# Attention's outputs stored in whole rows and put in order by the loads, in a hybrid decoder block

## The chip, the cores and the metric

The kernel runs on one core of a Trainium2 chip. The metric is the device time of one execution in microseconds; the median of several runs is compared. Five engines work side by side, each through its own list of instructions in order: PE (TensorE, matrix products), DVE (VectorE), ACT (ScalarE), POOL (GpSimd) and SP (SyncE), which in this kernel does nothing but issue DMA transfers. A transfer is carried out by the core's 16 DMA engines, in packets of one contiguous run of bytes each. An engine that needs another's result waits for a semaphore, and what stands behind the waiting instruction on the same engine waits with it.

## The reference

One block of a decoder for 1024 tokens of width 1024. An input projection feeds two groups of heads: eight heads of stick-breaking attention (64 wide) and four heads of a gated delta rule (128 wide). Both outputs are normed per head, gated, joined and multiplied by the output projection; the residual and a last norm follow.

```
def stick_breaking_attention(q, k, v):
    ...
        causal = s_idx[None, :] < t_idx[:, None]
        sp = jnp.where(causal, jax.nn.softplus(z), 0.0)
        tail = lax.cumsum(sp, axis=sp.ndim - 1, reverse=True) - sp
        attn = jnp.where(causal, jnp.exp(jax.nn.log_sigmoid(z) - tail), 0.0)
        outs.append(jnp.einsum('bhqk,bhkd->bhqd', attn.astype(v.dtype), vb))

def reference(x, norm1_w, w_in, ...):
        h = rmsnorm(x, norm1_w[layer])
        proj = jnp.einsum('btd,de->bte', h, w_in[layer])
        ...
        o_sb = rmsnorm(o_sb.transpose(0, 2, 1, 3), sb_norm_w[layer]).reshape(b, t_len, SB_WIDTH)
        o_sb = o_sb * jax.nn.silu(sb_z)
        qkv = jax.nn.silu(causal_depthwise_conv(jnp.concatenate([g_q, g_k, g_v], axis=-1), gdn_conv_w[layer]))
        ...
        o_gdn = gated_delta_chunked(gq, gk, gv, decay, beta)
        ...
        mixed = jnp.concatenate([o_sb, o_gdn], axis=-1)
        x = x + jnp.einsum('bte,ed->btd', mixed, w_out[layer])
    return rmsnorm(x, final_norm_w)
```

## The kernel before

**A planner lays out every queue.** While the kernel is built, `Model` (lines 174 to 345) keeps a clock of its own. Each instruction that the program records gets a price (`cost`, line 398), the instructions whose results it needs, and a rank `prio`: the lower, the sooner it is taken among those that are ready on its engine (`start`, line 301). A transfer costs SP 475 ns in this account, and its packets are priced by their length (line 404). The orders so found are fixed with dependencies at the end of `block`, so on the chip each engine keeps to the planner's order, whether or not the planner's times come true. Line 363 is the line of the helper that records, which is why nearly every row of the profile bears it; rows are told apart by their tiles. `interleave` (line 445) picks which of some twenty streams goes on next; each has a rank for its instructions (line 1638 on: DELTA 0, WEIGHTS 2, BANK 5, WINDOW 10, OUTPUT 12, RESULT 20).

**The stages.** First the queries and half of the values are projected straight from the loads. Then three things run interleaved on PE: the rest of the projections (`projections`, in the order of line 29), attention in windows of 256 tokens (`window`, line 1327: eight heads, four windows each), and the delta rule. After the projections and attention come the products with the output weights: first with the half of the weights that belongs to the delta rule (`products_delta`), then with that of attention (`products_attention`), each in eight blocks of 128 tokens.

**Attention's output.** A window ends with its output turned: 128 values (two partial sums of 64) by 256 tokens. VectorE adds the high and low halves (`o2`), transposes it in 32 by 32 squares into `oe` (line 1407; two buffers), and four stores (line 1409) finish the transposition by writing each square to its place in `o_s`, laid out token by token. Each store covers 32 partitions in runs of 128 bytes. The values of the next head, `v2a`, are loaded into a single buffer (line 1325), and the next head's `q2`, `kh`, `kl` likewise (line 1309).

**The end of attention.** `out_norm` (line 1415) loads a block of 128 tokens of all heads from `o_s` into `both`, 4 KB per token in one piece, for two blocks at a time (the fixed place sg3 cut in two); adds the two partial sums, squares, sums and raises to the power -0.5 on POOL with the tile `half`. `enter_attention` scales the block and gives the place back. `prepare(0)` has PE transpose the block, multiplies by the gate and splits it into a high and a low part (`mm`, shown as mmf); four of these fit. `products_attention` multiplies.

**Convolution.** `g_evac` (line 878) takes a projected bank of q, k or v of the delta rule, copies it with three columns ahead of it into `pre` (two buffers): zeros at the first half of the tokens, the last three columns of the first half at the second. Then come four taps, a sigmoid and a product. For heads 2 and 3 (TURNED is 2) the result is also transposed on VectorE into `pre` and stored by four transfers of 128-byte runs into `gt_s`. These transfers have the rank of the projections' stream, RESULT.

Of the kernel before, what the change touches and what calls it, by code (L numbers as in the profile page):

```python
# [10 lines left out]
F32 = mybir.dt.float32  # L11
F32R = mybir.dt.float32r
I32 = mybir.dt.int32
AF = mybir.ActivationFunctionType
# [3 lines left out]
P = 128  # L18
T = 1024
# [3 lines left out]
SBH = 8  # L23
# [10 lines left out]

OUT_WEIGHTS, DELTA, WEIGHTS, BANK, WINDOW, OUTPUT, RESULT, DECAYS = -1, 0, 2, 5, 10, 12, 20, 25


SAME = 130  # L40
# [438 lines left out]
def block(tc, xT_d, x_d, n1_d, wE_d, wQ_d, wC_d, conv_d, alog_d, dtb_d, mixw_d, wo_d, fnw_d, out_d):  # L479
    nc = tc.nc  # L480
    ck = Model({"V": nc.vector, "A": nc.scalar, "G": nc.gpsimd, "P": nc.tensor, "S": nc.sync})
    V, A, G, TE, S = ck.V, ck.A, ck.G, ck.P, ck.S

    with ExitStack() as top:
        top.enter_context(tc.manual_schedule(engines={mybir.EngineType.PE}))

        def open_pool(name, space="SB", ctx=top, before=(), **kw):
            if space != "SB":
                kw["space"] = getattr(bass.MemoryType, space)
            return Pool(ck, ctx.enter_context(tc.tile_pool(name=name, bufs=1, **kw)), space, before)  # L490

        fx = Fixed(ck, nc, {**{f"sg{w}": (2048 * (w + 1), 1) for w in range(4)}, "o2": (1024, 1), "kq": (4096, 4), "ak": (4096, 4)})
        cst = open_pool("cst")
        dr = open_pool("dr", "DRAM")
        ps = open_pool("ps", "PSUM")
# [12 lines left out]
        step = stepr.bitcast(F32)  # L508
# [4 lines left out]
        rstd = cst.tile([P, NB], F32, name="rstd")  # L513
        rs8 = cst.tile([P, NB], F32, name="rs8")
        ns8 = cst.tile([P, NB], F32, name="ns8")
        half = cst.tile([P, SBH], F32, name="half")
        V.memset(half, -0.5)
        norms = cst.tile([P, 2, 2, 4], F32, name="norms")
        root = cst.tile([P, 4], F32, name="root")
# [2 lines left out]
        def rsqrt(y, a, n):  # L522
            return G.tensor_tensor(y, a, half[:, 0:n], ALU.pow)
# [10 lines left out]
        gate_s = dr.tile([NK, P, T], F32, name="gate_s")  # L534
        g_s = dr.tile([GH, 3, P, T], F32, name="g_s")
        gt_s = dr.tile([GH, 3, T, P], F32, name="gt_s")
        o_s = dr.tile([T, SBH, P], F32, name="o_s")
        og_s = dr.tile([NB, P, GH, P], F32, name="og_s")
        rs_s = dr.tile([NB, P], F32, name="rs_s")
        cum_s = dr.tile([2, GH, NB, P], F32, name="cum_s")  # L540
# [83 lines left out]
        for tag, bufs in (("kh", 1), ("kl", 1), ("q2", 1), ("v2a", 1), ("sg2", 1), ("cc", 2), ("cc", 2), ("sg3", 1)):  # L624
            if tag[0] == "s":
                chl.append(fx.tile([P, 2, 520], F32R, "chl", tag))
            else:
                t = at_.tile([P, 1040 + (48 if tag == "kl" else 0)], F32R, tag=tag, bufs=bufs, name="chl")
# [15 lines left out]
        raw, loads = [], {}  # L644
        for k in range(NK):
            w = s0.tile([P, 512], F32, tag="wcr", bufs=6, name="wq")
# [76 lines left out]
        def first(f, *args, bank=BANK, **kw):  # L723
            ck.prio, prio = bank, ck.prio
            f(*args, **kw)
            ck.prio = prio
# [49 lines left out]
        flags = {}  # L776
# [101 lines left out]
        def g_evac(h, kind):  # L878
            wv = conv[:, 4 * kind + h, :]
            last = []  # L880

            def evac(pt, half):
                pre = gd.tile([P, 515], F32, tag="pre", bufs=2, name="pre")
                if half == 0:
                    V.memset(pre[:, 0:3], 0.0)
                else:
                    A.activation(pre[:, 0:3], last[0][:, 512:515], AF.Copy)
                last.append(pre)
                first(A.activation, pre[:, 3:515], pt, AF.Copy)
                ac = pr.tile([P, 512], F32, tag="kt", bufs=2, name="ac")  # L890

                first(A.activation, pt, pre[:, 0:512], AF.Copy, scale=wv[:, 0:1])
                for i in range(1, 4):
                    first(V.scalar_tensor_tensor, ac if i == 3 else pt, pre[:, i:i + 512], wv[:, i:i + 1], pt, ALU.mult, ALU.add)
                sg = pre[:, 0:512]
                first(A.activation, sg, ac, AF.Sigmoid)
                first(G.tensor_tensor, ac, ac, sg, ALU.mult)
                ts = slice(half * 512, half * 512 + 512)
                if h < TURNED:
                    return S.dma_start(g_s[h, kind, :, ts], ac)  # L900
                done = [S.dma_start(g_s[h, kind, :, ts], ac)] if kind < 2 else []
                first(V.transpose, sg, ac)
                turned = gt_s[h, kind, ts, :].rearrange("(b r) d -> r b d", r=32)
                return done + [S.dma_start(turned[:, :, 32 * a:32 * a + 32], sg[32 * a:32 * a + 32, :].rearrange("r (b c) -> r b c", c=32)) for a in range(4)]

            return evac

# [75 lines left out]
        def delta_pre():  # L983
            yield from decays(pre)
            for h in range(GH):
                for g in range(2):
                    u = 2 * h + g
                    yield from until(f"l{u}g")
                    yield from gdn_pre(h, g)
# [304 lines left out]
        def attention():  # L1294
            yield lambda: "v1" in flags and "dec" in flags
            for i in range(2):
                ccs.append(at_.tile([P, T + 1], F32, tag="cc", bufs=2, name="cc"))
                V.memset(ccs[i][:, T:T + 1], 0.0)
            for h in range(SBH):
                yield lambda: f"k{h // 2}" in flags  # L1300
                kh = at_.tile([P, 1040], F32R, tag="kh", name="kh")[:, 16:1040]
                kl = at_.tile([P, T], F32R, tag="kl", name="kl")
                q2 = at_.tile([P, T], F32R, tag="q2", name="q2")
                i, r = h // 2, slice((h % 2) * 64, (h % 2) * 64 + 64)
                loads = []

                twice = lambda a: a[r, :].unsqueeze(1).to_broadcast([SBD, 2, T])
                for t, src in ((q2, qk_s[i, :, r, :].rearrange("n d t -> d n t")), (kh, twice(qk_s[4 + i, 0])), (kl, twice(qk_s[4 + i, 1]))):
                    loads.append(S.dma_start(t.bitcast(F32), src.bitcast(F32)))
                hd[h] = (q2, kh, kl)  # L1310
                yield loads
                for w in range(4):
                    tok = f"w{w}"
                    yield lambda: busy[tok] == 0 and len([1 for v in busy if v[0] == "w" and busy[v]]) < WINDOWS
                    busy[tok] = 1
                    yield Stream(window(h, w, tok), 10 + 0.01 * (4 * h + w), WINDOW + 0.01 * (4 * h + w))
                    yield lambda: f"s{h}{w}" in flags
            yield lambda: f"e{SBH - 1}3" in flags
# [8 lines left out]
        def window(h, w, tok):  # L1327
# [3 lines left out]
            for i in range(2):  # L1331
                b = 2 * w + i
                end = (b + 1) * P
                sg = sg2[:, i, :]
                cc = ccs[i][:, T - end:T + 1]
                cuts = (0, 384, end) if end == 640 else (*range(0, end, 512), end)
                for s0, s1 in list(zip(cuts, cuts[1:]))[::-1]:
                    n = s1 - s0
# [19 lines left out]
            for j in range(w + 2):  # L1358
                if j <= w:
# [3 lines left out]
                    n = len(blocks)  # L1363
# [11 lines left out]
                    r = V.tensor_tensor(al, src, ah.bitcast(F32), ALU.subtract)  # L1375
# [13 lines left out]
                ahl, r = parts[j - 1]  # L1389
                ov2 = ov.rearrange("p (m t) -> p m t", m=2)  # L1390
                yield r
                for s in (2 * (j - 1), 2 * (j - 1) + 1):
                    i0 = 0 if s <= 2 * w else 1
                    c = slice(256 * (s % 2), 256 * (s % 2) + (1 if i0 else 2) * P)
# [7 lines left out]
            o2 = fx.tile([P, 256], F32, "o2", "o2")  # L1402
# [2 lines left out]
            busy["po"] = 0  # L1405
            oe = at_.tile([P, 256], F32, tag="oe", bufs=2, name="oe")
            V.transpose(oe, o2)
            rows_o = o_s[256 * w:256 * w + 256, h].rearrange("(b r) d -> r b d", r=32)
            flags[f"e{h}{w}"] = [S.dma_start(rows_o[:, :, 32 * a:32 * a + 32], oe[32 * a:32 * a + 32].rearrange("r (b c) -> r b c", c=32)) for a in range(4)]
            yield  # L1410


# [2 lines left out]
        def out_norm(n):  # L1415
            yield lambda: f"e{SBH - 1}3" in flags and fx.room("sg3")
            if n == 0:
                fx.part("sg3", 4096)
            for b in range(n, NB, 2):
                yield lambda: fx.room("sg3")  # L1420
                both = fx.tile([P, SBH, 2, SBD], F32, "both", "sg3")
                ck.hold(both)
                yield S.dma_start(both.rearrange("p h u d -> p (h u d)"), o_s[b * P:(b + 1) * P].rearrange("t h d -> t (h d)"))
                o, spare = both[:, :, 0, :], both[:, :, 1, :]
                V.tensor_tensor(o, o, spare, ALU.add)
                A.activation(spare, o, AF.Square)
                ss = at_.tile([P, SBH], F32, tag="oss", bufs=2, name="oss")
                V.tensor_reduce(ss, spare, AX.X, ALU.add)
                V.tensor_scalar(ss, ss, 1.0 / SBD, EPS, ALU.mult, ALU.add)
                rsqrt(ss, ss, SBH)  # L1430
                normed[b] = both, o, ss
                yield
# [203 lines left out]
        pre = Stream(delta_pre(), 0.7, DELTA + 0.7)  # L1636
# [43 lines left out]
```

## Time and profile before

| what | value |
|---|---|
| median of 3 runs | 636.03 us (634.78 to 637.17) |
| the profiled execution | 639.53 us |
| its span, first to last instruction | 637.8 us |
| mean granted clock of PE | 0.994 |
| DMA packets; mean rate | 165563; 188 GB/s |
| packets under 512 bytes | 96448 |
| share of the 16 engines' time on SP's queue | 62.3% |

The span lies inside the execution's time; the rest, 1.7 us, is ahead of the first and behind the last instruction. Rows give an engine, a line, an operation, the tile written and the tiles read (`o_s<-oe` is a transfer from the tile oe into o_s; a trailing f marks a tile at a fixed place). "SPq" is SP's issuing; a transfer's landing is told apart from it. PE's time is split in PE (products) and PEld (loading the stationary operand), which overlap. In PE's rows a matmul's end is modelled, so that neighbours overlap.

How the 16 DMA engines and the engines are filled over 40 slices of 16 us (tenths, 9 is 90% or more):

```profile
PE   8999999999999999999999989999999999999995
...
DVE  4379973322797798887797696777889774478754
ACT  6665567724786776775785866666777653232553
POOL 0124047728794696881679684386764325245522
...
DMA  8958337856557466598668768453652578984322
```

### The profile page before, as it was taken

How to read it: one execution, taken by the hardware profiler on the slowest of the kernel's cores; microseconds unless marked ns; L12 is line 12 of the kernel's file. 1: busy time of each engine (PE TensorE's matmuls, PEld its weight loads, DVE VectorE, ACT ScalarE, POOL GpSimd, SP SyncE). 2: the span in 40 equal slices, each digit the busy share in tenths (PEclk: the TensorE clock that was granted, in tenths of full speed). 3: DMA queues.
4: the chain of work that ended last, by engine and by line, in shares of the span. 5: the costliest groups of instructions: out<-in, count | busy, mean ns of one | idle time of the engine just before them, and what ended most of it. 6: DMA issues, size and time to landing. Idle time of an engine off the chain costs nothing.

```text
span 637.8 us, 11259 instructions
## 1 busy us (share of the span) xinstructions
PE 624.0 (98%) x3672; PEld 528.7 (83%) x3672; DVE 447.5 (70%) x810; ACT 393.9 (62%) x945; POOL 341.2 (53%) x429
## 2 busy tenths in 40 slices
PE   8999999999999999999999989999999999999995
PEld 7889988988888888788888777888888888888884
DVE  4379973322797798887797696777889774478754
ACT  6665567724786776775785866666777653232553
POOL 0124047728794696881679684386764325245522
PEclk9999999999999999999999999899999999999998
DMA  8958337856557466598668768453652578984322
GB/s 305 342 183 312 124 131 253 303 189 222 159 151 224 131 185 134 141 207 221 167 146 224 185 133 264 121 185 94 180 141 84 151 201 255 311 319 143 116 100 100
DMA packets 165563, 120.21 MB, mean 188 GB/s; under 512 B 96448, under 2 KB 131456, under 8 KB 165504
## 3 DMA queue, kind: packets, MB, share of 16 engines
q1 hardware_dynamic: 165216, 119.29, 62.3%
q8 instruction: 29, 0.48, 0.3%
q14 instruction: 30, 0.25, 0.1%
q10 hardware_dynamic: 288, 0.20, 0.1%
HBM read 80.22 MB, written 39.23 MB: 187 GB/s over the span
## 4 chain that ended last, share of the span: by engine, by line
PE 81%; DMA 6%; ACT 4%; DVE 3%; SPq 2%; issue 2%; POOL 1%; POOLq 0%; DVEq 0%; ACTq 0%
PE pp L363 52%; PE pz L363 21%; PE po L363 6%; PE pc L363 3%; SPq L363 2%; DVE cc L363 1%; DMA v2a<-v_s 1%; DMA kh<-qk_s 1%; DMA xr1f<-xT 1%; DMA o_s<-oe 1%; ACT sgf L363 1%; POOL ac L363 1%; DMA qk_s<-sqh 1%; ACT pz L363 1%; DMA cb<-cum_s 1%
## 5 line engine op out<-in xcount | busy, mean ns | idle before, releaser
L363 PE MATMUL pp<-xh,weh 128*128 128x512 f32 x360 | 146.4, 407 | 0.4 <-DVE ac L363 0.4
L363 PE MATMUL pp<-xh,wel 128*128 128x512 f32 x360 | 141.8, 394 | 0.0
L363 PE MATMUL pp<-xl,weh 128*128 128x512 f32 x360 | 141.3, 392 | 0.0
L363 POOL TENSOR_TENSOR sgf<-sgf,cc 128x128 f32<-128x128 f32 (+3 forms) x64 | 77.5, 1216 | 57.7 <-DVE cc L363 52.5
L363 POOL TENSOR_TENSOR wel<-wer,weh 128x512 fp32r<-128x512 f32 x48 | 62.5, 1305 | 72.0 <-ACT weh L363 71.6
L363 PEld LDWEIGHTS pp<-xh,wel 128*128 128x128 f32 x360 | 68.0, 189 | 15.3
L363 PEld LDWEIGHTS pp<-xh,weh 128*128 128x128 f32 x360 | 68.1, 189 | 12.8 <-DVE ac L363 0.9
L363 PEld LDWEIGHTS pp<-xl,weh 128*128 128x128 f32 x360 | 68.1, 189 | 11.5
L363 DVE TENSOR_TENSOR_SCAN cc<-pz,step 128x384 f32<-128x384 f32 (+2 forms) x64 | 53.4, 844 | 10.6 <-ACT pz L363 9.5
L363 ACT ACTIVATE sgf<-pz,rs 128x384 f32<-128x384 f32 (+3 forms) x96 | 53.5, 593 | 7.6 <-PE pz L363 7.6
L363 DVE TENSOR_TENSOR ahl<-pz,ahl 128x512 fp32r<-128x512 f32 (+1 forms) x80 | 49.5, 630 | 12.0 <-ACT ahl L363 11.3
L363 ACT ACTIVATE ahl<-pz 128x512 fp32r<-128x512 f32 (+1 forms) x80 | 43.2, 559 | 20.6 <-PE pz L363 20.1
L363 ACT ACTIVATE pz<-pz,ns 128x384 f32<-128x384 f32 (+3 forms) x96 | 52.5, 576 | 0.0
L363 PE MATMUL po<-ahl,v2a 128*128 128x512 f32 (+1 forms) x160 | 48.9, 400 | 2.4 <-DMA v2a<-v_s 2.3
L363 PE MATMUL pp<-wo,mmf 128*128 128x512 f32 x192 | 45.5, 396 | 0.0
L363 DVE SCALAR_TENSOR_TENSOR pp<-pre,conv,pp 128x512 f32<-128x512 f32 x42 | 31.4, 747 | 18.2 <-ACT pp L363 17.8
L363 PEld LDWEIGHTS pp<-wo,mmf 128*128 128x128 f32 x192 | 35.8, 188 | 8.4
L363 PE MATMUL pp<-woh,mmf 128*128 128x512 f32 (+2 forms) x136 | 41.9, 385 | 0.0
L363 DVE TENSOR_TENSOR_SCAN cc<-pz,cc,step 128x512 f32<-128x512 f32 (+1 forms) x32 | 38.8, 1211 | 4.1 <-ACT pz L363 3.0
L363 POOL TENSOR_TENSOR mmf<-mgf,mmf 128x512 fp32r<-128x512 f32 x16 | 21.9, 1366 | 37.0 <-ACT mmf L363 23.9
L363 POOL TENSOR_TENSOR ac<-ac,pre 128x512 f32<-128x512 f32 x24 | 31.0, 1293 | 16.3 <-ACT pre L363 10.9
L363 DVE TENSOR_TENSOR xr<-pp,xr 128x512 f32<-128x512 f32 (+2 forms) x33 | 22.2, 672 | 23.0 <-PE pp L363 23.0
(317 smaller groups left out, 1513.9 us busy)
## 6 DMA issues: line engine op xcount, KB each, us to landing
wer<-wE SPq DMA_DIRECT2D x48, 256.0 KB, 3.5
xr<-x SPq DMA_DIRECT2D x16, 512.0 KB, 7.6
g_s<-ac SPq DMA_DIRECT2D x20, 256.0 KB, 2.3
v_s<-v2e SPq DMA_DIRECT2D x16, 256.0 KB, 3.3
kqf<-g_s SPq DMA_DIRECT2D x16, 256.0 KB, 4.0
v2a<-v_s SPq DMA_DIRECT2D x8, 512.0 KB, 5.9
q<-qk_s SPq DMA_DIRECT2D x8, 512.0 KB, 4.5
kh<-qk_s SPq DMA_DIRECT2D x8, 512.0 KB, 3.9
```

Source lines behind the costliest of these rows:

```text
L363: ins = f(*args, **kw).ins
```

## The change

Five edits. (1) `o_s` becomes four windows by eight heads by 128 by 256, and a window's `oe` is stored in one transfer with rows of 1 KB; the squares are no longer put in their places there. (2) `out_norm` loads a block by four transfers, each into 32 partitions with runs of 128 bytes, which finish the transposition; the add behind them waits for all four. (3) The three columns of zeros in `pre` are written by ScalarE, as a copy of three zero columns of `step`, and no longer by VectorE's memset. (4) For heads 2 and 3 the stores of the convolved result and of its transposition get the rank STORES, 1. (5) The tile `half` moves to a fixed place of 32 bytes.

```
-OUT_WEIGHTS, DELTA, WEIGHTS, BANK, WINDOW, OUTPUT, RESULT, DECAYS = -1, 0, 2, 5, 10, 12, 20, 25
+OUT_WEIGHTS, DELTA, STORES, WEIGHTS, BANK, WINDOW, OUTPUT, RESULT, DECAYS = -1, 0, 1, 2, 5, 10, 12, 20, 25
...
-        fx = Fixed(ck, nc, {**{f"sg{w}": ...
+        fx = Fixed(ck, nc, {"half": (32, 1), **{f"sg{w}": ...
...
-        half = cst.tile([P, SBH], F32, name="half")
+        half = fx.tile([P, SBH], F32, "half", "half")
...
-        o_s = dr.tile([T, SBH, P], F32, name="o_s")
+        o_s = dr.tile([4, SBH, P, 256], F32, name="o_s")
...
                 if half == 0:
-                    V.memset(pre[:, 0:3], 0.0)
+                    A.activation(pre[:, 0:3], step[:, 0:3], AF.Copy)
...
                 if h < TURNED:
                     return S.dma_start(g_s[h, kind, :, ts], ac)
+                ck.prio, prio = STORES, ck.prio
                 done = [S.dma_start(g_s[h, kind, :, ts], ac)] if kind < 2 else []
                 first(V.transpose, sg, ac)
                 turned = gt_s[h, kind, ts, :].rearrange("(b r) d -> r b d", r=32)
-                return done + [S.dma_start(turned[:, :, 32 * a:32 * a + 32], sg[32 * a:32 * a + 32, :].rearrange("r (b c) -> r b c", c=32)) for a in range(4)]
+                done += [S.dma_start(turned[:, :, 32 * a:32 * a + 32], sg[32 * a:32 * a + 32, :].rearrange("r (b c) -> r b c", c=32)) for a in range(4)]
+                ck.prio = prio
+                return done
...
             V.transpose(oe, o2)
-            rows_o = o_s[256 * w:256 * w + 256, h].rearrange("(b r) d -> r b d", r=32)
-            flags[f"e{h}{w}"] = [S.dma_start(rows_o[:, :, 32 * a:32 * a + 32], oe[32 * a:32 * a + 32].rearrange("r (b c) -> r b c", c=32)) for a in range(4)]
+            flags[f"e{h}{w}"] = S.dma_start(o_s[w, h], oe)
...
-                yield S.dma_start(both.rearrange("p h u d -> p (h u d)"), o_s[b * P:(b + 1) * P].rearrange("t h d -> t (h d)"))
+                loads = []
+                for q in range(4):
+                    at = 32 * (4 * (b % 2) + q)
+                    loads.append(S.dma_start(both[32 * q:32 * q + 32].rearrange("p h u d -> p (h u d)").rearrange("p (n c) -> p n c", c=32),
+                                             o_s[b // 2, :, :, at:at + 32].rearrange("h (a r) c -> r (h a) c", r=32)))
+                yield loads
```

More of the change, by code (lines that the diff above doesn't have):

```diff
@@ L490, in open_pool @@
             return Pool(ck, ctx.enter_context(tc.tile_pool(name=name, bufs=1, **kw)), space, before)
-        fx = Fixed(ck, nc, {**{f"sg{w}": (2048 * (w + 1), 1) for w in range(4)}, "o2": (1024, 1), "kq": (4096, 4), "ak": (4096, 4)})
+        fx = Fixed(ck, nc, {"half": (32, 1), **{f"sg{w}": (2048 * (w + 1), 1) for w in range(4)}, "o2": (1024, 1), "kq": (4096, 4), "ak": (4096, 4)})
         cst = open_pool("cst")
```

## The prediction

> **What bounds the kernel now.** I read the page's head and its chain first, then PE's waits, then the stretches in which PE is not full.
>
> ```profile
> span 637.8 us, 11259 instructions
> ...
> PE 624.0 (98%) x3672; PEld 528.7 (83%) x3672; DVE 447.5 (70%) x810; ACT 393.9 (62%) x945; POOL 341.2 (53%) x429
> ...
> PE 81%; DMA 6%; ACT 4%; DVE 3%; SPq 2%; issue 2%; POOL 1%; POOLq 0%; DVEq 0%; ACTq 0%
> ```
>
> PE is busy for 624.0 of 637.8 us and holds 81% of the chain that ends last. The change removes no matmul, so at most 13.8 us of idle PE can be won, and not all of that. Where the idle time lies is told by the busy time by stretches (columns: PE, PEld, DVE, ACT, POOL, clock, DMA share, GB/s) and by PE's own waits:
>
> ```profile
> 360.00:400.00 40.00, 35.81 (x257) 29.48 (x258) 29.43 (x53) 26.93 (x75) 27.40 (x32) 0.98 0.77 207
> ...
> 600.00:638.00 38.00, 31.21 (x150) 25.53 (x148) 19.63 (x39) 17.68 (x39) 10.87 (x14) 0.95 0.24 97
> ...
> 398.00:400.00 2.00, 1.95 (x6) 1.66 (x7) 1.37 (x4) 1.98 (x6) 0.51 (x3) 0.65 1.07 289
> 400.00:402.00 2.00, 2.00 (x6) 1.52 (x6) 1.59 (x3) 2.00 (x6) 0.92 (x2) 0.50 0.85 237
> ...
> PE po L363 <- DMA v2a<-v_s: 2.3, 1, 2.3
> PE pz L363 <- ACT wy L363: 1.5, 1, 1.5
> PE pz L363 <- DVE cc L363: 0.6, 2, 0.4
> ```
>
> 6.8 us of it (38.00 - 31.21) is the end, in which the last rows are normed and written; the change does not touch that. 4.2 us (40.00 - 35.81) lie between 360 and 400: a wait of 2.3 for the values v2a of the next head and one of 1.5 for ScalarE. Just after the second the granted clock falls: 2 us at 0.65 and 2 us at 0.50 lose 2 x 0.35 + 2 x 0.50 = 1.7 us. So what a better order in the attention stage can win is about 2.3 + 1.5 + 1.7 + 0.6 = 6.1 us, 1% of the time. All else is matmuls back to back.
>
> [...]
>
> **The change part by part.** First the stores of attention's outputs and the queue in which they stand:
>
> ```profile
> L363 SPq DMA_DIRECT2D o_s<-oe x128: 302/448/2572, 177.3 to 522.9; - x128
> L363 SPq DMA_DIRECT2D bothf<-o_s x8: 320/332/422, 514.9 to 590.4; - x8
> ...
> 348.71 2.15 SPq L363 DMA_DIRECT2D o_s<-oe  x4
> 350.97 0.91 SPq L363 DMA_DIRECT2D gt_s<-pre  x2
> ...
> 356.56 1.00 SPq L363 DMA_DIRECT2D wer<-wE  x2
> 357.67 0.38 SPq L363 DMA_DIRECT2D vt<-gt_s  x1
> ...
> 361.34 0.43 SPq L363 DMA_DIRECT2D dt<-dt_s  x1
> 361.87 0.38 SPq L363 DMA_DIRECT2D v2a<-v_s  x1
> 362.46 4.11 SPq L363 DMA_DIRECT2D o_s<-oe  x4
> ...
> SPq L363 <- ACT pz L363: 1.5, 4, 0.6
> ```
>
> *Stores whole.* 128 stores become 32. That takes 96 issues x 0.448 = 43 us off SP between 177 and 523. The rows show SP issuing without a pause around 350 to 362, with v2a at the end of the file, so SP's queue is a resource in that stretch. Of the four stores at 348.71 three go: 3 x 0.448 = 1.3 us. Whether v2a gets them is open, since the weight loads (wer) at 356.56 wait for ScalarE with up to 0.6 us each time (last row), and time won ahead of such a wait is lost in it. Bounds of what PE gets: nothing, and the whole 2.3. The store's own wait for its transpose stays; behind it on SP wait fewer issues. The staging tile oe comes free after one landing, not after the fourth of four issues, 1.3 us sooner, which hides behind two buffers.
>
> *Packets.* What 128-byte packets cost is best seen where nothing else runs (a stretch of 2 us of the DMA view), 4 KB rows in a stretch of 3.6 us at the end:
>
> ```profile
> DMA packets 1989, 0.25 MB, mean 124 GB/s; under 512 B 1989, under 2 KB 1989, under 8 KB 1989
> ...
> q1 hardware_dynamic: 1989, 0.25, 72.2%
> ...
> DMA packets 144, 0.52 MB, mean 146 GB/s; under 512 B 16, under 2 KB 16, under 8 KB 144
> ...
> q1 hardware_dynamic: 144, 0.52, 41.3%
> ```
>
> 0.722 x 2 us x 16 engines / 1989 = 11.6 ns for a small packet; a block of 512 KB in 4 KB rows takes 0.413 x 3.6 = 1.5 us of all engines. The stores have 32 x 4 x 256 = 32768 small packets, 24 us of all engines spread over 345 us; 4096 rows of 1 KB take their place. How long a 1 KB packet takes no row here shows; between eight small ones (93 ns) and a quarter of a 4 KB row (1.5 us x 16 / 128 / 4 = 47 ns) it is 12 to 24 us; I take 12. The loads at the end then carry the 32768 small packets: 4096 a block, 3.0 us for 1.5 before.
>
> *Loads at the end.* 8 loads become 32. 24 more issues x 0.448 = 11 us of SP in a stretch where it is mostly idle. The nearest row for one is the scan's own 128-byte gather, of the same 128 KB:
>
> ```profile
> xc<-xd SPq DMA_DIRECT2D x4, 128.0 KB, 3.9
> ...
> bothf<-o_s SPq DMA_DIRECT2D x8, 512.0 KB, 6.2
> ...
> L363 DVE TENSOR_TENSOR mgf<-bothf,oss x8: 681/688/1781, 553.7 to 602.8; 128x512 f32<-128x512 f32 x8
> ...
> L363 POOL TENSOR_TENSOR mmf<-mgf,mmf x16: 1286/1292/2142, 531.7 to 610.8; 128x512 fp32r<-128x512 f32 x16
> ...
> 608.17 0.29 PE pz L363 x4
> 608.46 22.76 PE pp L363 x108
> ```
>
> Four issued 0.45 apart land at best after 3 x 0.45 + 3.9 = 5.3 us, 0.9 sooner than the 6.2 of now; one after another they take 15.6, 9.4 later. I take 2 later (1.35 for the issues and part of the 1.5 for the packets). Two places take turns, so blocks 2, 4 and 6 follow each other and the lateness adds three times: 6 us. The cover: the last block's split ends at 610.83 + 1.29 = 612.1, and PE comes to that block after three blocks of 5.67 us, at 608.46 + 17.0 = 625.5. That is 13.4 us of lead. The transposes that feed the split stand in PE's order at 608.17, but that order is laid out again with the loads' price in it. So I cost it at nothing; without the cover it would be 6 us.
>
> The add behind each load waits for all four. Behind it on VectorE stand the residual adds (xr<-pp) that free PE's two banks, so a late load stops PE within two products.
>
> *Zeros and turned stores.*
>
> ```profile
> L363 DVE MEMSET pre<- x12: 61/61/61, 76.3 to 337.2; 128x3 f32 x12
> ...
> L363 ACT ACTIVATE pre<-pre x12: 186/234/268, 81.7 to 356.0; 128x3 f32<-128x3 f32 x12
> ...
> L363 SPq DMA_DIRECT2D gt_s<-pre x48: 303/488/1761, 231.3 to 369.8; - x48
> ...
>   ACT pre L363: 0.8, 1
>   DVE pre L363: 0.7, 1
> ```
>
> VectorE loses 12 x 0.061 = 0.7 us, ScalarE gains 12 x 0.234 = 2.8 us, if a copy of zeros takes what the copy of the carried columns takes. ScalarE is 62% busy and PE has two banks in hand; nothing, or 2.8 if each one is exposed. The turned stores (48, and 8 beside them) get rank 1: in SP's order they now pass weight loads (rank 2) and everything of attention (rank 10 on). What they free is the buffer pre; the last two rows (who waited for gt_s) show 1.5 us of waiting on engines that are not the bound. Against that, one turned group of five ahead of a load delays it by 5 x 0.488 = 2.4 us. I take nothing for both. The tile half only moves.
>
> **Sum.** From 636.03 (median): stores, between 0 and -2.3 by the same order, and up to -6.1 if the new order loses both waits and the clock's dip; I take -2.0, most of one wait. Loads, zeros, turned stores: 0. Forecast 634.0. The profiled execution took 639.53 (its span 637.8 and 1.7 around it), 3.5 above the median, so I subtract from the median and not from the span.
>
> **The rivals.** (B) Every order on every queue is laid out anew from the planner's prices, and SP's file gets a quarter shorter; both waits and the dip go: 636.0 - 6.1 = 629.9. For it: v2a at the end of SP's file. Against: both waits are also tied to other transfers in front of them. (C) It is hidden anyway: SP's time is not what PE waits for, and the change does nothing: 636. For it: the waits of SP for other engines. (D) Slower: the 128-byte loads. From 13.4 / 3 = 4.5 us of lateness a block the lead is used up; at 6.5, midway between 4.5 and the bound of about 9, it is 3 x 6.5 - 13.4 = 6.1 us: 642. Against it: the 11.6 ns a packet. (E) A turned group ahead of a load of attention's inputs makes a new wait of 2.4 us, and the clock dips again for 1.7: 640.1.
>
> [...]
>
> **How the numbers follow.** Chances: forecast 0.42 (632.5 to 637), B 0.25, C 0.14, D 0.10, E 0.09. A measurement of this kernel tells about 0.5% from no change, 632.85 to 639.21. Faster: nearly all of B and a quarter of the forecast, 0.35. Slower: D and most of E, 0.18. Same: 0.47. The range reaches from a little beyond B, 628.0, to the middle of D, 641.5; some 0.12 is left out.
>
> **What would show it.** Right: 32 issues of o_s<-oe; v2a no longer in PE's list of waits, or under 1 us; a clock of 1.00 from 360 to 440; SP's waits grown by what its issues lost. Loads right: mgf<-bothf up to 10 us later than 602.8, PE without a gap from 540 to 631. D would show as VectorE waiting for bothf by several us and PE waiting in the last 60 us. E would show as a wait of PE for a DMA with gt_s issues just ahead of it on SP. Wrong altogether: PE's busy time itself changed by more than 2 us, since no matmul is touched.

## The result and the profile after

| kernel | median | runs | ratio to before, measured side by side (95%) |
|---|---|---|---|
| before | 636.6 us (634.78 to 637.80) | 4 | 1 |
| after | 645.19 us (641.78 to 650.64) | 4 | 1.013 (1.0092 to 1.0167) |

The change is slower by 1.3%; the forecast was 634.0 with a range of 628.0 to 641.5. The profiled execution of after took 641.78 us, the fastest of its four (the others had spans of 641.2, 644.8 and 648.5 us at mean clocks of 0.998, 0.99 and 0.987), and lies only 2.2 us above the profiled one of before where the medians differ by 8.6, so no trace of after shows the whole loss.

The head of the page and its chain, then PE's waits (who it waited for, us in total, times, longest), in the kernel after:

```profile
span 639.6 us, 11189 instructions
...
PE 622.2 (97%) x3672; PEld 528.5 (83%) x3672; DVE 448.3 (70%) x798; ACT 395.6 (62%) x957; POOL 342.2 (54%) x429
...
PE 68%; POOL 7%; DMA 6%; SPq 6%; issue 5%; DVE 4%; ACT 3%; POOLq 0%; ACTq 0%; DVEq 0%
```
```profile
PE pp L363 <- ACT bothf L363: 2.9, 1, 2.9
PE pp L363 <- DVE zt L363: 2.1, 1, 2.1
PE po L363 <- DVE step L363: 1.7, 1, 1.7
PE pz L363 <- DVE y L363: 1.2, 1, 1.2
PE pp L363 <- DVE v2e L363: 0.6, 1, 0.6
PE pz L363 <- ACT wy L363: 0.5, 1, 0.5
PE po L363 <- DMA v2a<-v_s: 0.5, 1, 0.5
```

PE does the same work (622.2 us), but its share of the chain falls from 81% to 68%. Of the waits of before, v2a is down from 2.3 to 0.5 and wy from 1.5 to 0.5, as hoped; 2.9, 2.1, 1.2 and 0.6 us stand at other places (the 1.7 for step is the start, which before has too). The busy time by stretches shows where, after first and then before:

```profile
360.00:400.00 40.00, 39.48 (x283) 32.54 (x282) 32.51 (x61) 29.20 (x76) 28.85 (x32) 1.00 0.79 236
280.00:320.00 40.00, 38.15 (x295) 32.70 (x296) 29.63 (x62) 27.24 (x79) 18.45 (x20) 1.00 0.51 131
520.00:560.00 40.00, 37.80 (x164) 30.19 (x163) 20.09 (x31) 9.24 (x16) 14.39 (x13) 1.00 1.07 251
560.00:600.00 40.00, 37.11 (x169) 29.91 (x168) 27.23 (x40) 13.18 (x22) 15.76 (x12) 0.96 0.91 183
```
```profile
280.00:320.00 40.00, 40.00 (x304) 33.91 (x303) 29.64 (x61) 26.47 (x79) 20.48 (x26) 1.00 0.75 195
520.00:560.00 40.00, 40.00 (x189) 33.01 (x189) 19.93 (x34) 11.66 (x29) 16.47 (x14) 1.00 0.90 276
560.00:600.00 40.00, 40.00 (x188) 32.38 (x187) 31.48 (x49) 15.18 (x26) 19.23 (x14) 1.00 0.57 199
```

Between 360 and 400 PE wins 3.67 us (39.48 against 35.81) and the clock's dip is gone. Three stretches that were full lose 1.85, 2.20 and 2.89 us, together 6.9; and the clock now falls in the last of them. The loss there can be followed. First the transfers by tile (min/median/max ns of an issue, first and last start) with what VectorE waited for, then SP's timeline (start, length, what), both of after:

```profile
L363 SPq DMA_DIRECT2D o_s<-oe x32: 320/338/1695, 177.0 to 512.0; - x32
L363 SPq DMA_DIRECT2D bothf<-o_s x32: 303/562/3475, 511.2 to 594.0; - x32
...
who waited for it (us, times):
  DVE bothf L363: 6.1, 4
```
```profile
550.89 3.41 SPq L363 DMA_DIRECT2D fnw<-fnw  x1
...
554.88 4.71 SPq L363 DMA_DIRECT2D bothf<-o_s  x4
...
567.00 7.77 SPq L363 DMA_DIRECT2D bothf<-o_s  x3
574.87 0.51 SPq L363 DMA_DIRECT2D worf<-wo  x1
575.47 3.82 SPq L363 DMA_DIRECT2D bothf<-o_s  x4
```

The stores have become what they should be. But issuing one of the new loads, 1024 packets of 128 bytes, holds SP for up to 3.5 us, and three of them take 7.77 us. Added up over the trace, the 32 loads cost SP 30.0 us, 0.94 each, where the forecast had 0.448. It is not the single transfer that takes so long: the quickest of the 32 was issued in 0.30 us, and fnw, which moves whole rows of 4 KB, held SP for 3.41 us here (0.63 in before). That it hangs on what is queued ahead fits these rows (with loads of 4 KB rows, in e1 below, fnw took 0.47 us and no load over 0.50); what it is in the queue that holds SP, no row shows. The last load of output weights (worf) goes out at 574.87, behind them. What follows from it, on VectorE, ScalarE and PE (timelines of after; in brackets the idle time before the row and what ended it):

```profile
577.00 0.69 DVE L363 TENSOR_TENSOR bothf<-bothf 128x512 f32<-128x512 f32 x1 [0.26 <-DMA bothf<-o_s]
580.28 1.28 DVE L363 SCALAR_TENSOR_TENSOR wol<-worf,mixw,woh 128x1024 fp32r<-128x1024 f32 x1 [2.59 <-ACT woh L363]
581.48 0.68 DVE L363 TENSOR_REDUCE oss<-bothf 128x8 f32<-128x512 f32 x1
582.99 0.69 DVE L363 TENSOR_TENSOR bothf<-bothf 128x512 f32<-128x512 f32 x1 [0.83 <-DMA bothf<-o_s]
583.60 0.17 DVE L363 TENSOR_SCALAR oss<-oss 128x8 f32<-128x8 f32 x1
583.67 0.69 DVE L363 TENSOR_TENSOR xr<-pp,xr 128x512 f32<-128x512 f32 x1
```
```profile
579.09 1.15 ACT L363 ACTIVATE woh<-worf,mixw 128x1024 fp32r<-128x1024 f32 x1 [1.62 <-DMA worf<-wo]
```
```profile
575.55 5.77 PE L363 MATMUL pp<-wo,mmf 128*128 128x512 f32 x24
581.16 0.46 PE L363 MATMUL pz<-step,mwf 128*128 128x128 f32 x4
584.50 0.47 PE L363 MATMUL pp<-woh,mmf 128*128 128x512 f32 x1 [2.89 <-ACT bothf L363]
```

VectorE stands idle 2.59 us for ScalarE's high part of the late weights, and 0.83 more for a late load; behind both stands xr<-pp, which frees PE's bank. PE fills its two banks from 575.55 on and has nowhere to write until xr ends at 583.67 + 0.69 = 584.36; it starts at 584.50. (The row names ScalarE's square of a block, which ended at about the same time and of which PE needs nothing.) Right behind it the clock is at half:

```profile
585.65:589.00 3.35, 3.35 (x10) 2.57 (x9) 1.94 (x2) 0.03 (x1) 1.28 (x1) 0.50 0.07 12
```

That shows where the time went in this execution. It does not yet show which edit sent it there.

### The profile page after: what moved, and what is told of

Read it like the earlier page. It is cut to its first block, busy times and chain, and to the rows that moved or that the text cites. A ratio compares the mean times of both kernels' runs of the same rounds, so it can differ in the third digit from the quotient of the medians.

```text
span 639.6 us, 11189 instructions
## 1 busy us (share of the span) xinstructions
PE 622.2 (97%) x3672; PEld 528.5 (83%) x3672; DVE 448.3 (70%) x798; ACT 395.6 (62%) x957; POOL 342.2 (54%) x429
## 4 chain that ended last, share of the span: by engine, by line
PE 68%; POOL 7%; DMA 6%; SPq 6%; issue 5%; DVE 4%; ACT 3%; POOLq 0%; ACTq 0%; DVEq 0%
PE pp L363 39%; PE pz L363 20%; PE po L363 6%; SPq L363 6%; PE pc L363 3%; POOL tt L363 2%; POOL ac L363 1%; POOL sgf L363 1%; DMA v2a<-v_s 1%; DMA vt<-g_s 1%; DMA og_s<-akf 1%; POOL wel L363 1%; DMA cb<-cum_s 1%; DVE ahl L363 1%; DMA bothf<-o_s 1%
## 5 line engine op out<-in xcount | busy, mean ns | idle before, releaser
L363 ACT ACTIVATE sgf<-pz,rs 128x384 f32<-128x384 f32 (+3 forms) x96 | 54.9, 591 | 3.7 <-PE pz L363 3.4
L363 PE MATMUL pp<-woh,mmf 128*128 128x512 f32 (+2 forms) x136 | 43.2, 396 | 2.9 <-ACT bothf L363 2.9
```

Source lines behind the costliest of these rows:

```text
L363: ins = f(*args, **kw).ins
```

## The experiments

Ratios are to the kernel before, run beside each kernel. The planner lays out every queue anew after almost any edit, so for each run it is said whether the order of the queues was held. Where it was, the instructions of every engine stand in the same order as in the kernel named, but for the operation that is exchanged.

**Which edits?** Four kernels with some of the edits (the diffs are against the kernel after), each in the order that the planner gives it. First stores and loads alone, edits 1 and 2 (e5):

```
-                    A.activation(pre[:, 0:3], step[:, 0:3], AF.Copy)
+                    V.memset(pre[:, 0:3], 0.0)
...
-                ck.prio, prio = STORES, ck.prio
...
-        half = fx.tile([P, SBH], F32, "half", "half")
+        half = cst.tile([P, SBH], F32, name="half")
```

> The kernel before with only attention's stores in rows of 1 KB and the loads in runs of 128 bytes. Theory 1: as slow as the changed kernel, 1.008 to 1.018, with the same late end. Theory 2: anything within 1% of before. Theory 3: as before, 0.996 to 1.004.

Measured: 635.17 us, 0.9971 (0.9958 to 0.9985). Slightly faster, with every 128-byte load in place and 31.5 us of SP for them. Then the other three edits alone, with the stores and loads of before (e4):

```
-            flags[f"e{h}{w}"] = S.dma_start(o_s[w, h], oe)
+            rows_o = o_s[256 * w:256 * w + 256, h].rearrange("(b r) d -> r b d", r=32)
+            flags[f"e{h}{w}"] = [S.dma_start(rows_o[:, :, 32 * a:32 * a + 32], oe[32 * a:32 * a + 32].rearrange("r (b c) -> r b c", c=32)) for a in range(4)]
```

> The changed kernel with attention's stores and loads put back as before: only the zeros on ScalarE, the rank of the turned stores and the place of the tile half remain. Theory 1: no slower than before, 0.993 to 1.004. Theory 2: anything within 1% of before, since it is yet another order. Theory 3: slower, 1.008 to 1.017.

Measured: 643.5 us, 1.009 (1.0061 to 1.0119): slower without a single small load at the end. The change without its rank, edit 4 (e8):

```
-                ck.prio, prio = STORES, ck.prio
```

> The changed kernel with the turned stores at their old rank. Theory A: still slow at the end, ratio 1.003 to 1.012. Theory B with the rank as what spoils the order: 0.995 to 1.003, and PE's wait for y near 281 us gone.

Measured: 641.48 us, 1.0051 (1.0025 to 1.0077). And the change without the zeros, edit 3 (e9):

```
-                    A.activation(pre[:, 0:3], step[:, 0:3], AF.Copy)
+                    V.memset(pre[:, 0:3], 0.0)
```

> The changed kernel with the zeros written by VectorE again. Theory A: still slow at the end, ratio 1.003 to 1.012. Theory B with the zeros as what spoils the order: 0.995 to 1.003, and PE's wait for y near 281 us gone.

Measured: 635.89 us, 0.996 (0.9936 to 0.9984). Read alone, these four seem to settle it: whatever has the zeros on ScalarE is slower, whatever has not is faster. What follows shows that this reading is wrong.

**Size of packets and place of the tile, order held.** In the order of after, the loads read 4 KB rows; the last step of the transposition is left out. So that the order stays, one more line, not printed here, has the planner price these loads as without the edit; e3 has the like (e1):

```
-                    loads.append(S.dma_start(both[32 * q:32 * q + 32].rearrange("p h u d -> p (h u d)").rearrange("p (n c) -> p n c", c=32),
-                                             o_s[b // 2, :, :, at:at + 32].rearrange("h (a r) c -> r (h a) c", r=32)))
+                    loads.append(S.dma_start(both[32 * q:32 * q + 32].rearrange("p h u d -> p (h u d)"),
+                                             o_s[b // 2].rearrange("h p t -> (h p t)").rearrange("(n f) -> n f", f=D)[P * (b % 2) + 32 * q:P * (b % 2) + 32 * q + 32]))
```

> The changed kernel with its order on every engine kept as it is; each of the 32 loads of attention's outputs still goes into 32 partitions, but reads 32 rows of 4 KB that lie together, so 1024 packets of 4 KB take the place of 32768 of 128 bytes. It leaves out the last step of the transposition (the rows come in a wrong order). Theory 1 (packets: at the end the small ones hold the DMA engines and SP, and everything queued there is late): the waits of PE near 535 and 581 and the clock's dip go, about 7 to 9 us, ratio to before 0.995 to 1.004. Theory 2 (the new order is worse by itself): ratio stays at 1.010 to 1.017. Theory 3 (zeros on ScalarE or the rank of the turned stores): stays at 1.010 to 1.017.

Measured: 638.83 us, 1.0019 (0.9996 to 1.0042); the loads cost SP 11.9 us in place of 30.0. In this order, and with the tile `half` where the change puts it, the small packets cost 1.1% (1.013 - 1.0019). The converse, in the order of before: the stores leave gaps in `o_s`, so that its eight loads consist of 32768 packets of 128 bytes (e3):

```
-        o_s = dr.tile([T, SBH, P], F32, name="o_s")
+        o_s = dr.tile([T, SBH * 4, 64], F32, name="o_s")
...
-                yield S.dma_start(both.rearrange("p h u d -> p (h u d)"), o_s[b * P:(b + 1) * P].rearrange("t h d -> t (h d)"))
+                yield S.dma_start(both.rearrange("p h u d -> p (h u d)").rearrange("p (n c) -> p n c", c=32), o_s[b * P:(b + 1) * P, :, 0:32])
```

> The kernel before with its order on every engine kept; attention's outputs lie in memory with a gap of 128 bytes after each run of 128, so that its 8 loads at the end move the same data in 32768 packets of 128 bytes, in one issue a block and not four. Nothing is left out. Theory 1: 5 to 10 us slower than before, ratio 1.007 to 1.016, with waits of PE between 540 and 600. Theories 2 and 3: as before, 0.997 to 1.003. If the four issues a block and not the packets are the harm, also 0.997 to 1.003.

Measured: 638.6 us, 1.0028 (1.0008 to 1.0048). As many packets of the same size cost 0.3% here. That is not yet a difference between two orders, because here the tile `half` is not moved, and a packet took 12.9 ns where one in after took 16.7. Now only the tile `half` goes back to its pool, in the order of after (e6):

```
-        half = fx.tile([P, SBH], F32, "half", "half")
+        half = cst.tile([P, SBH], F32, name="half")
```

> The changed kernel with the tile half back in its pool; every engine keeps its order. It shifts all fixed places (the one that attention's outputs are loaded into among them) back by 32 bytes. Theory A (place: with the shift a 128-byte packet into that place takes longer, 16.7 ns in the changed kernel's profile for 13.0 in the run with the stores and loads alone): packets after 500 us back to 13 ns, the waits of PE near 535 and 581 gone or under 1 us, ratio to before 0.997 to 1.005. Theory B (order: small packets meet the full DMA engines in this order): ratio 1.009 to 1.017, packets at 16 ns or more.

Measured: 640.92 us, 1.0056 (1.003 to 1.0082). Half of the loss goes with a tile of 32 bytes. PE's wait behind bothf is nearly gone; the one behind zt is as long as in after:

```profile
PE pp L363 <- DVE zt L363: 2.1, 1, 2.1
...
PE pp L363 <- ACT bothf L363: 0.3, 1, 0.3
```

The tile is first among the fixed places, so all others move by 32 bytes, `both` among them. Over the 36864 packets of 128 bytes after 500 us (32768 of them go into `both`), one took 16.7 ns on average in after and 13.1 in this run. With the tile back, the small packets cost the order of after 0.4% (1.0056 - 1.0019, if the tile's place does nothing to rows of 4 KB), as near e3's 0.3% as these intervals can tell. And the reverse, stores and loads alone (e5, in its order) with the tile at the fixed place (e7):

```
-        half = cst.tile([P, SBH], F32, name="half")
+        half = fx.tile([P, SBH], F32, "half", "half")
```

> The kernel before with attention's stores in 1 KB rows, the 128-byte loads and the tile half at its fixed place; every engine keeps the order of the run with stores and loads alone (0.997). Theory A: packets after 500 us at 15 to 18 ns, 3 to 8 us slower than that run, ratio to before 1.002 to 1.010. Theory B: 0.995 to 0.999.

Measured: 637.19 us, 0.9971 (0.9946 to 0.9996), the ratio of e5, though its packets took 17.5 ns in place of 13.2. So packets that are slower by a quarter to a third cost 0.7% in one order and, to within 0.3%, nothing in another. The price of the tile's place hangs on the order.

**Is it the order?** Two theories from here on. O: the zeros cost nothing themselves; they make the planner lay out another order, and orders differ by about a per cent. Z: the zeros on ScalarE cost time. The test of O is to change the order and nothing else, by one price in the planner. Before, with VectorE's price off by 0.5% (g6):

```
-    return (130 if name == "scalar_tensor_tensor" and isinstance(args[2], bass.AP) else 69) + 1.04 * n
+    return (130 if name == "scalar_tensor_tensor" and isinstance(args[2], bass.AP) else 69) + 1.035 * n
```

> The kernel before with one price of the planner changed by 0.5% (VectorE 1.035 ns an element instead of 1.04): the same instructions, but every queue is laid out anew, about as much as by the change itself. Theory O (what the zeros, the rank and the moved tile do, they do by the new order alone, and orders differ by about 1% among themselves): somewhere between 630 and 644 us, off 637 by 0.3% or more, with PE waits of 1 to 3 us at other places than before. Theory Z (zeros on ScalarE cost by themselves): within 0.3% of the kernel before, 635 to 639.

Measured: 650.38 us, 1.0189 (1.0145 to 1.0233). The instructions of before, none changed, and a loss no smaller than that of the change. PE's longest waits of this run, and the stretch at half clock:

```profile
PE pz L363 <- DVE cc L363: 5.0, 1, 5.0
PE pz L363 <- DVE dt L363: 1.9, 1, 1.9
PE pp L363 <- DVE ac L363: 1.8, 1, 1.8
```
```profile
365.70:379.20 13.50, 8.13 (x21) 5.98 (x22) 12.55 (x22) 5.14 (x12) 11.32 (x9) 0.50 0.64 168
```

PE waits 5.0 us, from 362.36 to 367.35; the clock falls at 365.64, within that wait, and stays at half for 13.65 us. Next before, with SP's issue at 490 ns in place of 475, which changes about half as much of the order (g7):

```
-            cost = 475
+            cost = 490
```

> The kernel before with SP's issue priced at 490 ns instead of 475: the same instructions, about half as much of the order changed as by the change. Theory O: 630 to 644, and not the same as the run with VectorE's price. Theory Z: within 0.3% of the kernel before, 635 to 639.

Measured: 636.85 us, 0.9998 (0.997 to 1.0026): no difference, so not every new order is worse. The change itself with the same edit of the price (g8):

> The changed kernel with SP's issue priced at 490 ns instead of 475: all five edits stay, the order is another. Theory O: the loss is that of one order, so this comes anywhere from 634 to 646, and the waits of 2.9 us (bank behind bothf) and 2.1 us (bank behind zt) are not both there. Theory Z: it stays slower by 0.5 to 1.5%, 640 to 646.

Measured: 640.09 us, 1.0041 (1.0017 to 1.0065): two thirds of the loss are gone with all five edits in place. These two runs do not part the theories: 636.85 lies in the range of both, and 640.09 in O's and just inside Z's. And stores and loads alone with VectorE's price at 1.045 (g9):

```
-    return (130 if name == "scalar_tensor_tensor" and isinstance(args[2], bass.AP) else 69) + 1.04 * n
+    return (130 if name == "scalar_tensor_tensor" and isinstance(args[2], bass.AP) else 69) + 1.045 * n
```

> The two edits of the stores and loads alone, with VectorE priced at 1.045 ns an element instead of 1.04: the same instructions as in the run of those two edits (635.2 us), in another order. Theory O: off that by 0.3% or more either way, 630 to 642. Theory Z: within 0.3% of it, 633.5 to 637.

Measured: 641.88 us, 1.0059 (1.0025 to 1.0093). The edits that gave 0.9971 are slower in this order. In g6 and g9 fails what Z took for granted, that an order alone moves the time by no more than 0.3% (it had 635 to 639 and 633.5 to 637). O was itself too modest: g6 lies beyond its 644. Neither run has zeros on ScalarE, so what these cost is settled only by the next two.

**Crossing zeros and order.** The planner lays out the queues as if VectorE wrote the zeros, and each of the 12 copies is then put into ScalarE's queue at the moment that the planner had for it. This gives the instructions of after in the order of e9 (h1):

```
+    def set_zeros(out):
+        ins = nc.scalar.activation(out, step[:, 0:3], AF.Copy).ins
+        op = ck.record("V", ins, [out], [], 69 + 1.04 * 3, None)
...
+        for op in zeros:
+            ck.order["V"].remove(op)
+            to = ck.order["A"]
+            to.insert(next((n for n, o in enumerate(to) if o.at > op.at), len(to)), op)
```

> All five edits, in the order of the run without the zeros' edit (635.9 us, 0.996): the planner lays out the queues as if VectorE wrote the zeros, and then each of the 12 copies is put into ScalarE's queue at the moment at which the planner had VectorE write it. The same instructions as in the changed kernel, in another order. Theory O (the order): 633 to 639, as the run without the zeros' edit. Theory Z (zeros on ScalarE cost by themselves): 640 to 646.

Measured: 635.74 us, 0.9972 (0.9951 to 0.9993). The other way, the order of after with the zeros by VectorE (h2, the same edit with the engines exchanged):

```
-        ins = nc.scalar.activation(out, step[:, 0:3], AF.Copy).ins
-        op = ck.record("V", ins, [out], [], 69 + 1.04 * 3, None)
+        ins = nc.vector.memset(out, 0.0).ins
+        op = ck.record("A", ins, [out], [step[:, 0:3]], 93 + 3 / 1.2, None)
```

> The crossing of the run before this one: the order of the changed kernel (645.2 us), laid out as if ScalarE wrote the zeros, with the 12 zeros then written by VectorE at the same moments. The same instructions as in the run without the zeros' edit. Theory O: 641 to 648, as the changed kernel. Theory Z: 634 to 639.

Measured: 645.15 us, 1.0105 (1.0073 to 1.0137).

| zeros by | order of e9 | order of after |
|---|---|---|
| VectorE | 0.996 (e9) | 1.0105 (h2) |
| ScalarE | 0.9972 (h1) | 1.013 (after) |

Down a column the intervals overlap; along a row they lie 1.4 to 1.6% apart. The rows show it too. PE's longest waits in h2, then PE's waits, the loads' rows and the stretch from 560 to 600 in h1:

```profile
PE pp L363 <- DVE zt L363: 4.3, 2, 2.5
PE pp L363 <- ACT bothf L363: 3.2, 1, 3.2
```
```profile
PE pp L363 <- DVE xr L363: 1.5, 2, 1.1
PE pz L363 <- DVE y L363: 1.2, 1, 1.2
PE pz L363 <- issue: 1.2, 1, 1.2
```
```profile
L363 SPq DMA_DIRECT2D bothf<-o_s x32: 303/798/6187, 514.5 to 593.2; - x32
...
who waited for it (us, times):
...
  DVE bothf L363: 7.0, 4
```
```profile
560.00:600.00 40.00, 37.27 (x170) 29.32 (x169) 29.50 (x47) 15.18 (x28) 19.04 (x13) 1.00 0.85 175
```

h2 has the waits of after without its zeros. And h1 has loads that are worse than those of after: one holds SP for 6.2 us, and VectorE waits 7.0 us for them instead of 6.1. PE does feel it: between 560 and 600 it loses 2.73 us in h1 (40.00 - 37.27), nearly the 2.89 of after, though in waits of at most 1.2 us. What h1 lacks are the other losses of after: it loses nothing from 280 to 320 or from 520 to 560, and its clock stays at 1.00 from 560 to 600.

**A faster version.** Edits 1, 2 and 4 alone, in the order of e9 (f4):

```
-        half = fx.tile([P, SBH], F32, "half", "half")
+        half = cst.tile([P, SBH], F32, name="half")
```

> Edits 1, 2 and 4 (stores, loads, rank), without the zeros and with the tile half in its old place: the order of the run without the zeros' edit. Theory O: it keeps the 635.9 us of that run, and gains up to 0.5% where the packets into both get faster (from 16.0 ns to about 13): 632.5 to 636.5. Theory Z says the same of it. If the moved tile has no price where the end has slack: 635 to 637.

Measured: 634.72 us, 0.9962 (0.9941 to 0.9983), against 0.996 with the moved tile (packets 13.2 and 16.0 ns): again the tile's place costs nothing that shows in this order. e9 with SP's issue priced at 480 ns, which changes the order about as much as the change did (of VectorE's 810 instructions, 463 keep their sequence; from before to after it was 447) (f3):

```
-            cost = 475
+            cost = 480
```

> Edits 1, 2, 4 and 5 without the zeros', with SP's issue priced at 480 ns instead of 475: the same instructions as in the run without the zeros' edit (635.9 us), nearly the whole order another. Theory O: off 635.9 by 0.3% or more, between 632 and 646. Theory Z: within 0.3%, 634 to 638.

Measured: 632.76 us, 0.993 (0.9908 to 0.9951), lower than e9's 0.996 by the order alone, though the two intervals still meet. And all five edits in that order, h1 with the same price (h3):

```
-            cost = 475
+            cost = 480
```

> All five edits, with the 12 zeros by ScalarE, in the order of the run without the zeros' edit and with SP priced at 480 ns (632.8 us, 0.993). Theory O: 631 to 636, faster than both kernels, with the very instructions of the changed kernel, which took 645.2. Theory Z: 640 to 646.

Measured: 633.25 us, 0.9938 (0.9917 to 0.9959). The instructions of after, which took 645.19 us, 12 us sooner and faster than before. PE's list of waits in it, whole but for those under 0.6 us:

```profile
PE po L363 <- DVE step L363: 1.7, 1, 1.7
PE pp L363 <- DVE xr L363: 1.6, 2, 0.9
PE pz L363 <- issue: 0.6, 1, 0.6
```

## Why the prediction was wrong

**The step that failed** is the sum: "stores, between 0 and -2.3 by the same order, and up to -6.1 if the new order loses both waits and the clock's dip", and next to it "Loads, zeros, turned stores: 0". That the order is laid out anew was written down, but only as a gain (rival B), with a single wait of 2.4 us and one dip of the clock against it (rival E, chance 0.09). The loads were put at nothing for a cover that belongs to the order of before; in the order of after the small packets cost 1.1%. In truth the order is the largest term and has both signs. Kernels with the same instructions, in the orders measured: before 1.0, 0.9998 and 1.0189; stores and loads 0.9971 and 1.0059; e9's 0.996, 0.993 and 1.0105; the change 1.013, 1.0041, 0.9972 and 0.9938. These runs spread from -0.7 to +1.9%, and a forecast that knew of it would have needed a range about as wide; 641.5 as its end was too near.

**Stores whole.** Right: 32 issues of 0.338 us, v2a at 0.5 us, the clock 1.00 from 360 to 440, both waits down to 0.5 us and the dip gone as in B. Forecast -2.0; e5, the two edits alone, gave -0.3%, some 1.8 us; but g9 shows that this too is one order's number.

**Packets.** A packet of 1 KB took 50 ns on average between 177 and 523, so the 12 us taken for the stores was right. For 128 bytes the forecast had 11.6 ns; it was 13.1 to 13.3 where the tile stays, 14.9 to 17.5 where it is moved. A block is 4096 x 16.7 ns / 16 = 4.3 us of all engines and not 3.0.

**Loads at the end.** 24 more issues were costed at 0.448 us from the rows of the stores; the new ones took 0.94 on average and up to 3.5. That SP has "a stretch where it is mostly idle" was true before and is not after: between 554 and 583 SP issues for 25.2 us where it was 5.2, and the weights behind the loads come late. That a late load stops PE by way of VectorE's queue and the residual adds was named (0.83 of the 3.4 us that VectorE waited); that the loads hold up other transfers on SP, the other 2.59, was not. The cover of 13.4 us was read off the order of before, for the last block alone; PE lost its time from 581.6 to 584.5, with 55 us to go, and not at the end of the lead, where D put its price. D's signs are there (VectorE waits 6.1 us for bothf, PE waits in the last 60 us), and with a chance of 0.10 it came nearest to the time; but e5 has the same loads and is faster than before, so the loads alone do not make D's 642. (The midpoint that D names is 6.75 and not 6.5; with it D would be 642.9.) That mgf<-bothf would come up to 10 us later was right (610.5 for 602.8); PE without a gap from 540 to 631 was not. In the order of after the small packets cost 1.1% (e1), or 0.4% with the tile back; in that of before, where the tile is not moved, 0.3% (e3).

**Zeros.** Costed at nothing, and at one order they cost nothing that shows: the intervals of the three pairs (0.996 and 0.9972, 1.0105 and 1.013, 0.993 and 0.9938) overlap, though ScalarE is the slower each time, by 0.1 to 0.25%. What they did was to move the planner to another order.

**The tile half "only moves".** Wrong: it moves `both` by 32 bytes and the small packets slow down from 13.1 to 16.7 ns. In the order of after that is 0.7% (e6); in those of e5 and e9 it is nothing that shows. Why the packets slow down stays open.

**Rank.** Left open. The run without it (1.0051) has another order, and no run held the order while taking the rank away; a rank acts through the order alone.

**What of the 1.3% is explained.** In the order of after, 1.1% goes with the small packets, about two thirds of that with the tile's 32 bytes, and all of it with another order. These are not parts to be added: they are ways to give one tight place more room. Why the planner's order of after is tight there was not taken further. Its account has every issue at 475 ns, while these took 940; that this misleads it fits the timeline but was not tried.

## What to carry to other kernels

Where a planner or scheduler lays out the whole program, an edit has two effects, its own and that of a new order, and the second can be several times the first: hold the order to measure an edit, and change nothing but the order (one price by half a per cent) to learn how much a single timing is worth before blaming an edit. Two versions that differ by one edit and by their whole order say nothing of the edit, however often they are timed and however neatly four of them line up. And a cover that hides a cost belongs to one order: the same shift by 32 bytes cost 0.7% in one order and nothing that shows in two others.

## What the runs showed of the hardware

How long SP takes to issue a transfer is not set by the transfer alone. 1024 packets of 128 bytes took it from 0.30 to 3.5 us in after (0.94 on average) and up to 6.2 us in h1; the same 128 KB in 4 KB rows took 0.37 us on average (11.9 / 32, e1). In e3 the same 32768 packets in eight issues cost SP 8.1 us, in the 32 issues of after 30.0, though in another order and with the tile `half` in another place.

A shift of 32 bytes in the place on the chip made transfers of 128 bytes slower: 13.1 to 13.3 ns on average in four runs without it (e5, e6, f4, g9), 14.9 to 17.5 in all nine with it, and at one order 27% (after against e6), 33% (e7 against e5) and 21% (e9 against f4). Not every packet is slower: the median is 13 ns in after and in e6, but 30% of the packets take longer than that in after and 3% in e6, and 12% in after take 26 ns or more, twice the median. Why only some are slowed, no run here shows.

Inside these kernels (the fall at each one's end left aside) the falls of the clock lasted once, twice or four times the same length: 3.41 us at half in after (585.63 to 589.05) and in before (398.61 to 402.02), 6.83 in e6, g7 and h2, 13.65 = 4 x 3.41 in g6. No one length of wait goes with them: the wait ahead of the fall was 2.9 us in after and 1.5 in before, and in g7 the clock fell at 396.22 with PE busy for 7.95 of the 8 us from 388 to 396. Nor did every wait bring a fall: behind that of 2.1 us at 536 in after there was none. What sets it off stays open. In g6 PE was busy for 8.13 of 13.50 us at half clock, so the fall cost about 4 us there, an estimate (half of the busy time; in after products of 512 columns started every 0.43 us during the fall and every 0.23 us right behind it).
